# A row-maximum kernel that ignores NaN: ScalarE writes back part of each tile from the 31st to the 60th, and the last tiles are divided anew

## The chip, the cores and the metric

The kernel runs on one core of one Trainium2 chip. The metric is the device time of one execution in microseconds (us). A core has several engines that work side by side and wait for each other by semaphores: ScalarE (ACT in the profile), GpSimd (POOL), VectorE (DVE) and SyncE (SP), which here only issues transfers. TensorE is not used.

## What is computed

```python
def setup_inputs():
    batch, seq, dim = 32, 2048, 2048
    x = np.random.randn(batch, seq, dim).astype(np.float32)
    mask = np.random.rand(batch, seq, dim) < 0.1
    x[mask] = np.nan
    return {"x": x, "axis": -1}

def reference(x, axis):
    return np.nanmax(x, axis=axis).astype(np.float32)
```

There are 65536 rows of 2048 float32 values, a tenth of them NaN. The output is the largest value of each row with the NaNs left out. The input is 537 MB, the output 0.26 MB.

## The kernel before

**How the work is cut.** Each of the 128 partitions gets 512 rows. A unit of 512 values, a quarter of a row (`Q`), is the measure of everything: a partition has 2048 of them. They are worked on in 74 tiles; the first has 4 quarters, each other one 28 (seven rows). This text counts tiles from 1. The list `TILES` has one entry for each tile, with three lists in quarters:

- the loads: `[20, 8]` means that the tile comes by two transfers, of 20 and 8 quarters. Each load has 128 rows, one for each partition, and is issued by SyncE (line 316).
- the pieces, by which the NaNs are taken out. An entry is one ScalarE instruction that makes keys; a tuple is one key instruction whose result is then worked on in several parts. A positive number is written back by GpSimd, a negative one by ScalarE.
- the reduces: each is one instruction of VectorE over so many quarters.

So `([28], [7, 9, 12], [16, 12])` is one load, three keys, three write-backs by GpSimd and two reduces (of four rows and of three), and `([28], [9, 12, -7], [8, 20])` gives the last 7 quarters to ScalarE and reduces two rows and then five.

**What is done to a piece.** ScalarE reads the upper 16 bits of each float32 as an integer and makes a key from it by a Prelu (`kt<-xt`, line 222): the key of a NaN is such that the way back gives the upper half of minus infinity. The write-back computes `TOP - key` and stores it over the upper half, by GpSimd's tensor_scalar (`xt<-kt`, line 232) or by a ScalarE Copy (`xt<-kt`, line 222). The lower half stays where it is, so every number is as it was and every NaN is minus infinity. VectorE then takes the maximum over whole rows (line 239). A reduce that ends within a row leaves its value in the last element it read, and the next one, which waits for it, begins there:

```python
                            lo = done - 1 if done % D else done
```

**Buffers.** A tile lies in one of three buffers `xt`; the loads of a tile wait for the last reduce of the tile three before (`free`). Keys lie in three buffers `kt` of 12 quarters each. A piece that no longer fits goes to the next key buffer and waits until everything in it has been written back; if it is also the last piece of its tile, it waits for the buffer after that too:

```python
                        if at + c == sum(loads) * Q:

                            kold = kold + last(kfree[(key + 1) % NKEYS])
```

**Order of the work.** Every engine works in the order of the program, tile after tile, and waits only by semaphores. SyncE issues the loads in order, each on the next of 14 lanes; a lane's load also waits for the one that used it before. ScalarE does the key of a piece and then the write-backs that are held for it. A negative piece is written back at once after its own key; one that is written as a float (`-7.0`) is held until after the next key, except where it is the tile's last:

```python
                            held.append((at - c, at, key, kp, e_key, piece))
                            if not wait or at == sum(loads) * Q:
                                release()
```

Where a reduce needs one last piece from GpSimd and one from ScalarE, and nobody else needs these, both count up one semaphore (`joints`, a pair), and the reduce waits for it alone; tiles 70 to 73 have no such pairs (`APART`).

**The end.** The tiles form six groups (15, 15, 15, 15, 13 and 1 tiles), each with its own stretch of the output. After tile 60 one VectorE instruction (line 245, over 414 values of each partition) turns minus infinity into NaN for the rows of the first four groups; after tile 74 one does the last group's 7 values, and two GpSimd instructions (lines 260 and 274) do the fifth group's. SyncE then stores the six groups.

Of the kernel before, what the change touches and what calls it, by code (L numbers as in the profile page):

```python
# [20 lines left out]
    + [([28], [9, 12, -7], [8, 20])]  # L21
    + [([28], [7, 9, 12], [16, 12])] * 7
    + [([28], [9, 12, -7], [8, 20])]
    + [([28], [7, 9, 12], [16, 12])] * 7
    + [([28], [9, 12, -7], [8, 20])]
    + [([28], [7, 9, 12], [16, 12])] * 7
    + [([28], [9, 12, -7], [8, 20])]
    + [([28], [7, 9, 12], [16, 12])] * 7
    + [([28], [6, 10, 12], [16, 12])] * 3
    + [([28], [7, 9, 12], [16, 12])]  # L30
    + [([28], [6, 10, 12], [16, 12])] * 3
    + [([28], [7, 9, 12], [12, 16])] * 2
    + [([28], [7, 10, 11], [12, 16])]
    + [([28], [6, 10, 12], [16, 12])] * 3
    + [([28], [8, 11, 9], [8, 8, 12])]
    + [([20, 8], [11, -6, 6, 5], [16, 12])]
    + [([20, 8], [12, (-4, 7), 5], [8, 8, 12])]
    + [([17, 11], [12, (-4, 6), 6], [4, 12, 12])]
    + [([16, 12], [11, -5, 5, 7], [16, 12])]
    + [([13, 15], [9, -4, 7, 8], [12, 8, 8])]  # L40
    + [([14, 14], [9, -4, 4, 4, 7], [12, 8, 8])]
    + [([11, 10, 7], [5, 6, (-3, 7), 7], [4, 4, 4, 8, 8])]
    + [([11, 9, 8], [4, 7, (-2, 7), 6, -2], [4, 4, 4, 8, 8])]
    + [([8, 7, 6, 7], [3, 5, 7, (3, -3), 3, 4], [8, 4, 8, 8])]
    + [([6, 5, 6, 5, 6], [5, (5, -1), (-1, 5), 5, 3, 3], [4, 4, 4, 4, 4, 4, 4])]
    + [([5, 6, 5, 4, 4, 3, 1], [(-2, 3), 3, 3, (4, -1), 4, 4, -2.0, 2], [4, 4, 3, 1, 4, 4, 4, 4])]
    + [([4, 4, 3, 2, 4, 2, 3, 3, 3], [2, 2, 4, (-2.0, 1), 2, 3, 3, (-1, 2), (1, -1, 1), 2, -1.0], [4, 4, 4, 4, 4, 4, 4])]
)

GROUPS = [TILES[i : i + 15] for i in range(0, 60, 15)] + [TILES[60:73], TILES[73:]]  # L50
# [453 lines left out]
```

## Time and profile before

| | |
|---|---|
| median of 3 runs | 1252.54 us (1252.48 to 1253.04) |
| the profiled execution | 1252.48 us, its span 1250.7 us |
| loads | 105, 536.87 MB read, 429 GB/s over the span |
| DMA queue busy | 99.4% of the span |
| VectorE (DVE) | 1111.4 us busy, 179 instructions |
| ScalarE (ACT) | 965.6 us busy, 273 instructions |
| GpSimd (POOL) | 1168.5 us busy, 242 instructions |
| ScalarE's keys wait for loads | 257.9 us in 69 waits |
| VectorE waits for GpSimd | 128.1 us in 58 waits |
| last load landed, last reduce ended | 1242.24 us, 1247.91 us after the span's start |

Busy time is the sum of an engine's instructions, and a wait is idle time of an engine that ended when another engine or a load was done. The span runs from the first instruction of the program to the last; the execution's own time has 1.8 us beside it. A line of the groups or the timeline has the engine, the line of the helper that issues the instruction, what it writes and reads, and the shape; a timeline line merges neighbouring instructions of one kind (`x2`), gives their start and their time, and in brackets the idle time before them with what ended it.

### The profile page before, as it was taken

The numbers are of one execution on the slowest core, as the hardware profiler recorded it, in microseconds if no ns is written. First come the engines' busy times: TensorE is split into PE (matmuls) and PEld (weight loads), VectorE is DVE, ScalarE is ACT, GpSimd is POOL, SyncE is SP. The second block draws the span as 40 slices with busy tenths as digits, with TensorE's granted clock in tenths as the row PEclk, the third lists the DMA queues.
The fourth block names the chain that finished last, engine by engine and source line by source line (L and its number), as shares of the span: only waits on it lengthen the run. The fifth ranks groups of instructions, "written<-read, shape, count | busy, mean of one in ns | idle before, by whom it ended". The sixth has DMA issues, their size and how long they took to land.

```text
span 1250.7 us, 891 instructions
## 1 busy us (share of the span) xinstructions
DVE 1111.4 (89%) x179; ACT 965.6 (77%) x273; POOL 1168.5 (93%) x242
## 2 busy tenths in 40 slices
DVE  0888989888889888898988888998888899999999
ACT  3777887778777877788777877777777778999997
POOL 2999989998999899998999899999999999989998
DMA  9999999999999999999999999999999999999997
GB/s 415 440 418 433 440 440 438 413 440 440 440 433 418 440 440 438 429 424 440 440 436 424 431 440 438 436 424 433 440 438 435 422 436 436 425 434 429 431 428 301
DMA packets 15991, 537.20 MB, mean 430 GB/s; under 512 B 2544, under 2 KB 2544, under 8 KB 3568
## 3 DMA queue, kind: packets, MB, share of 16 engines
q1 hardware_dynamic: 15984, 537.14, 99.4%
q14 instruction: 7, 0.06, 0.0%
HBM read 536.87 MB, written 0.26 MB: 429 GB/s over the span
## 4 chain that ended last, share of the span: by engine, by line
DMA 40%; DVE 29%; POOL 22%; ACT 9%; issue 1%; SPq 0%
DMA xt<-in_x_dram 40%; DVE acc L239 29%; POOL xt L232 22%; ACT kt L222 8%; ACT xt L222 1%; SPq L316 0%; DVE acc L245 0%; SPq L499 0%; SPq L215 0%
## 5 line engine op out<-in xcount | busy, mean ns | idle before, releaser
L232 POOL TENSOR_SCALAR xt<-kt 128x3584 int16<-128x3584 uint16 (+11 forms) x236 | 1167.4, 4947 | 77.6 <-ACT kt L222 63.9
L239 DVE TENSOR_REDUCE acc<-xt 128x3 f32<-128x6144 f32 (+4 forms) x175 | 1107.5, 6379 | 135.6 <-POOL xt L232 128.1
L222 ACT ACTIVATE kt<-xt 128x3584 uint16<-128x3584 int16 (+9 forms) x247 | 913.4, 3734 | 278.0 <-DMA xt<-in_x_dram 257.9
L222 ACT ACTIVATE xt<-kt 128x512 int16<-128x512 uint16 (+6 forms) x24 | 52.8, 2202 | 0.7
L245 DVE SCALAR_TENSOR_TENSOR acc<-acc 128x414 f32<-128x414 f32 (+1 forms) x2 | 2.2, 1111 | 0.1
L222 ACT ACT_TABLE_LOAD x1 | 1.3, 1283 | 0.9 <-SPq L215 0.9
L239 DVE TENSOR_REDUCE xt<-xt 128x1 f32<-128x1536 f32 x1 | 1.7, 1743 | 0.0
L278 DVE MEMSET scalars<- 128x1 f32 x1 | 0.1, 59 | 1.0 <-SPq L215 1.0
L260 POOL TENSOR_SCALAR late<-acc 128x91 int32<-128x91 f32 x1 | 0.5, 549 | 0.1
L274 POOL TENSOR_TENSOR acc<-acc,late 128x91 int32<-128x91 int32 x1 | 0.3, 341 | 0.1
L485 POOL MEMSET const-float32-0.0<- 128x1 f32 x1 | 0.1, 98 | 0.2 <-issue 0.2
L222 ACT ACTIVATE scalars<-scalars 128x1 f32<-128x1 f32 x1 | 0.2, 203 | 0.0
L485 POOL MEMSET const-bfloat16-1.0<- 128x1 bf16 x1 | 0.1, 101 | 0.0
L485 POOL MEMSET const-uint8-127<- 128x1 uint8 x1 | 0.1, 101 | 0.0
L485 POOL MEMSET const-float32-1.0<- 128x1 f32 x1 | 0.1, 98 | 0.0
## 6 DMA issues: line engine op xcount, KB each, us to landing
xt<-in_x_dram SPq DMA_DIRECT2D x61, 7168.0 KB, 22.6
xt<-in_x_dram SPq DMA_DIRECT2D x2, 5120.0 KB, 17.4
xt<-in_x_dram SPq DMA_DIRECT2D x3, 2816.0 KB, 22.7
xt<-in_x_dram SPq DMA_DIRECT2D x4, 2048.0 KB, 22.3
xt<-in_x_dram SPq DMA_DIRECT2D x5, 1536.0 KB, 29.1
xt<-in_x_dram SPq DMA_DIRECT2D x2, 3584.0 KB, 24.8
xt<-in_x_dram SPq DMA_DIRECT2D x6, 1024.0 KB, 26.8
xt<-in_x_dram SPq DMA_DIRECT2D x3, 1792.0 KB, 30.1
```

The costliest lines, as they stand in the source:

```text
L222: lambda: nc.scalar.activation(**kw),
L232: lambda: nc.gpsimd.tensor_scalar(**kw),
L239: return order.add("dve", nc.vector, lambda: do(**kw), deps)
L245: lambda: nc.vector.scalar_tensor_tensor(out=acc, in0=acc, scalar=LEAST, in1=acc, op0=ALU.is_ge, op1=ALU.mult,),
L260: lambda: nc.gpsimd.tensor_scalar(out=none, in0=acc, scalar1=LEAST, scalar2=float(0x00400000), op0=ALU.is_lt, op1=ALU.mult,),
L274: lambda: nc.gpsimd.tensor_tensor(out=bits, in0=bits, in1=none, op=ALU.add),
L278: e_warm = order.add("dve", nc.vector, lambda: nc.vector.memset(warm, 1.0), [])
L485: nc = _bacc.Bacc("TRN2", target_bir_lowering=False, num_devices=1)
```

## The change

Only the list `TILES` is changed. There are again 74 tiles of the same sizes and the same groups.

- Tiles 31 to 38 become `[10, 12, -6]` with reduces `[8, 20]`, tiles 39 to 61 `[9, 12, -7]` with `[8, 20]` or `[4, 24]` (13 of them the latter): ScalarE writes back the last 6 or 7 quarters. Tiles 33 and 41 had `[9, 12, -7]` before. Some of the numbers are floats.
- Tiles 62 to 74 are divided into other pieces, other reduces and other loads. The loads of the whole kernel go from 105 to 118; tile 63 comes by one load instead of two, tiles 73 and 74 by 14 each instead of 7 and 9, some of them of one quarter (256 KB). The reduces of tiles 63 to 74 go from 52 to 58; tile 74 has 13 instead of 7, among them six rows that are reduced in two steps.

```diff
--- before.py
+++ after.py
@@ -21,30 +21,41 @@
     + [([28], [9, 12, -7], [8, 20])]
     + [([28], [7, 9, 12], [16, 12])] * 7
     + [([28], [9, 12, -7], [8, 20])]
-    + [([28], [7, 9, 12], [16, 12])] * 7
+    + [([28], [7, 9, 12], [16, 12])] * 5
+    + [([28], [10, 12, -6.0], [8, 20])] * 2
+    + [([28], [10, 12, -6], [8, 20])]
+    + [([28], [10, 12, -6.0], [8, 20])] * 2
+    + [([28], [10, 12, -6], [8, 20])]
+    + [([28], [10, 12, -6.0], [8, 20])]
+    + [([28], [10, 12, -6], [8, 20])]
+    + [([28], [9, 12, -7], [4, 24])]
+    + [([28], [9, 12, -7], [8, 20])] * 2
+    + [([28], [9, 12, -7], [4, 24])]
+    + [([28], [9, 12, -7.0], [8, 20])]
+    + [([28], [9, 12, -7], [4, 24])]
+    + [([28], [9, 12, -7.0], [4, 24])] * 3
+    + [([28], [9, 12, -7.0], [8, 20])]
+    + [([28], [9, 12, -7.0], [4, 24])]
+    + [([28], [9, 12, -7.0], [8, 20])] * 2
+    + [([28], [9, 12, -7.0], [4, 24])] * 4
+    + [([28], [9, 12, -7.0], [8, 20])] * 2
+    + [([28], [9, 12, -7.0], [4, 24])]
+    + [([28], [9, 12, -7], [4, 24])]
+    + [([28], [9, 12, -7.0], [8, 20])]
     + [([28], [9, 12, -7], [8, 20])]
-    + [([28], [7, 9, 12], [16, 12])] * 7
-    + [([28], [9, 12, -7], [8, 20])]
-    + [([28], [7, 9, 12], [16, 12])] * 7
-    + [([28], [6, 10, 12], [16, 12])] * 3
-    + [([28], [7, 9, 12], [16, 12])]
-    + [([28], [6, 10, 12], [16, 12])] * 3
-    + [([28], [7, 9, 12], [12, 16])] * 2
-    + [([28], [7, 10, 11], [12, 16])]
-    + [([28], [6, 10, 12], [16, 12])] * 3
-    + [([28], [8, 11, 9], [8, 8, 12])]
-    + [([20, 8], [11, -6, 6, 5], [16, 12])]
-    + [([20, 8], [12, (-4, 7), 5], [8, 8, 12])]
-    + [([17, 11], [12, (-4, 6), 6], [4, 12, 12])]
-    + [([16, 12], [11, -5, 5, 7], [16, 12])]
-    + [([13, 15], [9, -4, 7, 8], [12, 8, 8])]
-    + [([14, 14], [9, -4, 4, 4, 7], [12, 8, 8])]
-    + [([11, 10, 7], [5, 6, (-3, 7), 7], [4, 4, 4, 8, 8])]
-    + [([11, 9, 8], [4, 7, (-2, 7), 6, -2], [4, 4, 4, 8, 8])]
-    + [([8, 7, 6, 7], [3, 5, 7, (3, -3), 3, 4], [8, 4, 8, 8])]
-    + [([6, 5, 6, 5, 6], [5, (5, -1), (-1, 5), 5, 3, 3], [4, 4, 4, 4, 4, 4, 4])]
-    + [([5, 6, 5, 4, 4, 3, 1], [(-2, 3), 3, 3, (4, -1), 4, 4, -2.0, 2], [4, 4, 3, 1, 4, 4, 4, 4])]
-    + [([4, 4, 3, 2, 4, 2, 3, 3, 3], [2, 2, 4, (-2.0, 1), 2, 3, 3, (-1, 2), (1, -1, 1), 2, -1.0], [4, 4, 4, 4, 4, 4, 4])]
+    + [([28], [8, (4, -7.0), 9], [12, 16])]
+    + [([28], [5, 7, 10, 6], [4, 8, 8, 8])]
+    + [([16, 12], [(8, -4), 8, 8], [12, 8, 8])]
+    + [([12, 16], [(9, -3.0), 8, 8], [12, 8, 8])]
+    + [([16, 12], [(8, -4), 8, 8], [12, 8, 8])]
+    + [([13, 15], [8, -5, 8, 7], [12, 8, 8])]
+    + [([14, 14], [6, (-3, 5), 6, 8], [4, 8, 8, 8])]
+    + [([10, 12, 6], [(-3, 7), 5, (5, -1.0), 7], [8, 4, 8, 8])]
+    + [([9, 6, 5, 8], [8, 7, -5, 4, 4], [8, 12, 8])]
+    + [([7, 8, 6, 7], [(5, -2), (1, 2), 5, (-2, 4), 3, 4], [8, 4, 4, 8, 4])]
+    + [([5, 4, 7, 5, 4, 3], [5, (1, -3), 3, 4, 5, (2, -2.0), 3], [8, 4, 4, 4, 4, 4])]
+    + [([5, 2, 2, 1, 4, 1, 1, 2, 2, 2, 3, 1, 1, 1], [4, 3, (1, -1, -1.0), 3, 3, (-1.0, 3), 2, 2, (-1, 3)], [4, 4, 4, 4, 4, 4, 4])]
+    + [([3, 2, 3, 3, 2, 4, 1, 1, 1, 1, 1, 4, 1, 1], [2, 3, 3, 2, (-2, 1), 1, 1, 2, (1, 1, -1.0), 2, 2, (-1, 1, 1), -1.0], [2, 2, 1, 3, 4, 3, 1, 2, 2, 2, 2, 2, 2])]
 )
 
 GROUPS = [TILES[i : i + 15] for i in range(0, 60, 15)] + [TILES[60:73], TILES[73:]]
```

## The prediction

> **What bounds the kernel now.** I read the page first: busy shares and the rate of the loads.
>
> ```profile
> DVE 1111.4 (89%) x179; ACT 965.6 (77%) x273; POOL 1168.5 (93%) x242
> GB/s 415 440 418 433 440 440 438 413 440 440 440 433 418 440 440 438 429 424 440 440 436 424 431 440 438 436 424 433 440 438 435 422 436 436 425 434 429 431 428 301
> q1 hardware_dynamic: 15984, 537.14, 99.4%
> ```
>
> The load queue is never idle. 28 quarter rows (7.34 MB) take a steady 16.9 us, 0.604 us a quarter. So for most of the run nothing that the engines do can matter unless it takes over 16.9 us a tile or frees a buffer too late. The table by windows of 16.9 us shows where that changes (window, busy us of DVE, ACT and POOL with instructions, clock, DMA share, GB/s):
>
> ```profile
> 980.20:997.10 16.90, 15.14 (x3) 12.40 (x4) 16.44 (x4) 1.00 1.00 434
> 1081.60:1098.50 16.90, 16.90 (x5) 15.38 (x5) 16.13 (x4) 1.00 1.02 438
> 1216.80:1233.70 16.90, 16.87 (x10) 16.12 (x13) 16.27 (x9) 1.00 1.02 426
> 1233.70:1250.60 16.90, 14.38 (x8) 11.15 (x11) 11.84 (x11) 1.00 0.51 198
> ```
>
> VectorE is idle 1.8 us a window in the middle and not at all near the end. The timeline of the end says from when:
>
> ```profile
> 1032.58 2.06 DVE L245 SCALAR_TENSOR_TENSOR acc<-acc 128x414 f32<-128x414 f32 x1
> 1034.56 23.79 DVE L239 TENSOR_REDUCE acc<-xt 128x4 f32<-128x8192 f32 x4
> 1058.51 162.84 DVE L239 TENSOR_REDUCE acc<-xt 128x3 f32<-128x6144 f32 x40 [0.16 <-POOL xt L232]
> 1223.04 24.87 DVE L239 TENSOR_REDUCE acc<-xt 128x1 f32<-128x513 f32 x12
> 1247.94 0.17 DVE L245 SCALAR_TENSOR_TENSOR acc<-acc 128x7 f32<-128x7 f32 x1
> ```
>
> From tile 61's first reduce (1034.56) to the last (1247.91) VectorE stops for under 0.4 us. The last load lands at 1242.24, 5.7 us before. So: loads set the time up to tile 60, VectorE's unbroken row of reduces after it. The chain of waits at the end runs through GpSimd (1203.99 to 1236.83), but VectorE's idle time there is nil: the two are level.
>
> The third thing to read is what one tile of the new form costs; tile 9 already has it (9 and 12 quarters by GpSimd, 7 by ScalarE):
>
> ```profile
> 141.07 9.26 ACT L222 ACTIVATE kt<-xt 128x4608 uint16<-128x4608 int16 x2 [4.07 <-DMA xt<-in_x_dram]
> 145.19 12.46 POOL L232 TENSOR_SCALAR xt<-kt 128x4608 int16<-128x4608 uint16 x2 [1.02 <-ACT kt L222]
> 150.56 3.19 ACT L222 ACTIVATE kt<-xt 128x3584 uint16<-128x3584 int16 x1 [0.23 <-POOL xt L232]
> 153.78 4.20 ACT L222 ACTIVATE xt<-kt 128x3584 int16<-128x3584 uint16 x1
> 157.95 7.12 ACT L222 ACTIVATE kt<-xt 128x3584 uint16<-128x3584 int16 x2
> 158.02 10.82 DVE L239 TENSOR_REDUCE acc<-xt 128x5 f32<-128x10240 f32 x1 [1.46 <-ACT xt L222]
> 161.22 16.73 POOL L232 TENSOR_SCALAR xt<-kt 128x3584 int16<-128x3584 uint16 x3 [3.56 <-ACT kt L222]
> ```
>
> **Part 1: tiles 31 to 61.** -7 and -7.0 give the same order, since a last piece is always written back at once; 33 and 41 had ScalarE write back before, so 29 tiles change. (Times below count from the tile's landing, L.)
>
> ScalarE: 9.26 for the first two keys, 0.23 waiting for GpSimd to free a key buffer, 3.19, 0.03, 4.20: done at L+16.91. A following key can start 0.13 before a write-back ends (2.49 from 1093.42, next key at 1095.78), so 16.78 a tile against a load's 16.90. A 10, 12, -6 tile: 4.46 for the key of 10, then 6.04 until GpSimd's 10 quarters (5.90) are done, 2.76, 0.03, 3.63, less 0.13: 16.79. ScalarE just keeps up, at 99%. GpSimd falls from 16.7 to 12.5 a tile, worth nothing while the loads bind.
>
> VectorE: the work is the same; what matters is when the buffer comes free. 8, 20: the 20 starts at L+16.95 and ends at L+27.8 (now, with 16, 12: 118.34 - 90.25 = L+28.1). 4, 24: the 24 is not in the trace; 10.82 plus one row of 2.13 is 12.96, so L+29.9. The load three tiles on is issued then, with 33.8 - 29.9 = 3.9 us of the load before it still to come. The first load of the run needed 5.67 - 0.96 = 4.71 us from issue to landing, of which four quarters' transfer is 2.41: a lead of 2.3 us is enough. 3.9 covers it; uncovered, each of the 13 such tiles would cost what is missing. Part 1: 0.
>
> ScalarE: Activation LUTs of the Trainium skill (What ACT_TABLE_LOAD costs) gives an ACTIVATE 186 ns and 0.833 ns an element, by which the write-back of 3584 takes 3.17 and the tile 15.8, with a microsecond of slack. The row's 4.20 disagrees and decides; by either the loads bind.
>
> **Part 2: the hand-over, tiles 60 to 62.** Tile 59 (landing 987.34) ends on VectorE at 1017.2; tile 60's 8 runs to 1021.5, its 20 to 1032.3, the flag operation (2.06) to 1034.3, tile 61's 8 to 1038.6. Tile 61's 20 needs ScalarE at 1021.12 + 16.9 = 1038.0, so it runs 1038.6 to 1049.3 (before: 1049.69). Tile 62 (landing 1038.00): keys 8 and 11 end at 1046.4; the key of 9 waits for GpSimd's 8 (1041.72 + 4.77 = 1046.49) and ends at 1050.6; GpSimd's 9 ends at 1056.04. VectorE's 12 runs 1049.3 to 1055.8, its 16 from 1056.1 to 1064.8. Tile 63 starts about 1064.72 instead of 1065.07: **-0.35**.
>
> **Part 3: tiles 63 to 74 on VectorE.** The rows reduced are the same; their number goes from 52 to 58. Start to start, 8 quarters take 4.32 and two of 4 take 2 x 2.19, so a cut costs 0.06: 6 x 0.06 = **+0.36**. A row done in two reduces makes the second wait for the first: it starts 0.03 after the first's end (1223.01, 1223.04), where others start 0.085 before it. Six such rows against one: 5 x 0.115 = **+0.58**. That sum holds while the other two stay ahead. Going through these tiles with ACT, POOL and DVE durations by size, GpSimd is done with what VectorE needs next 0.2 to 1.5 us early nearly everywhere; the tightest are tile 62's 16 (above), tile 70's 8 (1170.8 against 1170.7) and, in tile 74, leads of 0.25 to 0.4. GpSimd's last piece ends about 1246.0, ScalarE's at 1245.8, VectorE's last reduce starts about 1247.2. GpSimd's relief (4.2 us of work fewer after tile 60) thus ends as idle time in tiles 66, 67, 70 and 72, where it waits for keys.
>
> **Part 4: thirteen more loads.** Landing to landing, one load takes 16.88 (tile 62), two 16.94 to 16.97, five 17.07, nine 17.25: 0.046 a load, 0.6 in all, so the last lands at about 1242.8. VectorE's row covers that with some 1 us; if the cover were gone, at most 0.6. The 13 issues on SP (0.43 each) sit behind the wait for tile 70's and 71's buffers, free at 1186 and 1201.5, needed at 1208 and 1225. SP stalled up to 5.16 us in such an issue (1202.01), with nine loads outstanding; nine of the new ones are still 14 quarters, 8 us of transfer. The four early stores follow later, but only after the last load, as now.
>
> Sum on the profiled run (1252.48 us; span 1250.7 and 1.8 around it): -0.35 + 0.36 + 0.58 = +0.6. The median of the runs is 1252.54, the same within 0.1. **Forecast 1253.1 us**, no difference by the 0.2% (2.5 us) that a measurement can tell.
>
> **Rivals.**
> - ScalarE becomes the pace in tiles 31 to 61 (slower). If back to back the next key starts 0.08 after the write-back instead of 0.13 before (that gap is GpSimd's), a tile takes 16.99, and 31 tiles lag 2.8 us; VectorE's 20 or 24 waits for it, so tile 62 starts that much later and all follows: 1252.5 + 0.6 + 2.8 = 1255.9. It decides above 16.90 a tile. For: 99% load, no two such tiles in a row in the trace. Against: the 0.13 overlap occurs after every write-back with its load landed. 0.10.
> - 4, 24 frees buffers too late: half a microsecond short in 13 tiles is 6.5 us, 1259.6. Against: 3.9 against 2.3. 0.03.
> - Each extra load pays its own latency (the 2.3 above less overlap, at least 1.3): 13 x 1.3 = 17 us, 1270. Against: nine loads cost 0.37 in tile 74. 0.02. DMA: Bandwidth & Descriptors of the Trainium skill (Rules for kernel authors) asks for 1 MiB or more per DMA; the new loads of one quarter are 256 KB. The one such load before landed 0.63 after its neighbour against 0.60, so by this trace the rule costs little in a full queue.
> - The end follows the last landing, VectorE having more slack than I see (faster): 1242.8 + key 0.61, write-back 0.78, a half-row reduce 1.2 and gaps is 1245.5, 2.4 before: 1250.0. For: the chain runs through GpSimd, which is relieved. Against: VectorE's unbroken row. 0.05.
>
> **Chances.** Forecast 0.80, mostly within 0.2%. Faster 0.04 (most of the last rival), same 0.81, slower 0.15 (the first three). Range: a microsecond and a half below for stops of the loads (16.99 to 17.38 us in a few tiles) that may fall otherwise, up to most of the first rival above: 1251.5 to 1255.3.
>
> **What would show it.** ScalarE's keys in tiles 40 to 60 starting on a landing, not on its own queue; tile 62's last reduce ending near 1064.8; VectorE without idle time after it; the last landing near 1242.8. Wrong if VectorE waits over a microsecond in tiles 63 to 74, or tile 61 lands past 1023.

## The result, and the profile after

The changed kernel takes 1258.38 us (median of 6 runs, 1256.79 to 1260.71) against 1252.47 (1252.40 to 1253.04): the ratio is 1.0049, with a 95% interval of 1.0037 to 1.0061. It is slower by 5.9 us, more than the 0.2% that was named, and outside the range of the prediction. The profiled execution is the slowest of the six: 1260.71 us, span 1258.9.

The page of the changed kernel, the lines that answer to those of before:

```profile
DVE 1115.6 (89%) x184; ACT 1086.4 (86%) x306; POOL 1050.6 (83%) x221
GB/s 412 437 437 435 434 415 435 438 438 437 434 421 428 437 437 437 437 435 437 434 423 428 437 437 434 432 430 430 428 423 426 437 434 404 432 435 428 427 423 261
q1 hardware_dynamic: 17856, 537.14, 99.1%
```

GpSimd's 118 us less and ScalarE's 121 us more are as the change says. VectorE has 4.2 us more. Line numbers of the changed kernel are 11 higher than before (L233 here is L222 there). The table by windows of the changed kernel:

```profile
980.20:997.10 16.90, 12.99 (x3) 16.63 (x5) 12.37 (x3) 1.00 1.00 434
1081.60:1098.50 16.90, 16.90 (x5) 14.78 (x5) 16.58 (x5) 1.00 1.03 445
1216.80:1233.70 16.90, 16.90 (x8) 15.85 (x15) 16.16 (x10) 1.00 1.03 420
1233.70:1250.60 16.90, 16.76 (x13) 15.86 (x16) 15.79 (x15) 1.00 0.83 327
```

VectorE is as full at the end as before, only later. The timeline of the changed kernel around tiles 60 and 61 has ScalarE's part as forecast and one line that was not:

```profile
1007.09 9.26 ACT L233 ACTIVATE kt<-xt 128x4608 uint16<-128x4608 int16 x2
1016.59 3.19 ACT L233 ACTIVATE kt<-xt 128x3584 uint16<-128x3584 int16 x1 [0.24 <-POOL xt L243]
1019.81 4.21 ACT L233 ACTIVATE xt<-kt 128x3584 int16<-128x3584 uint16 x1
1024.66 9.26 ACT L233 ACTIVATE kt<-xt 128x4608 uint16<-128x4608 int16 x2 [0.65 <-DMA xt<-in_x_dram]
1028.79 12.46 POOL L243 TENSOR_SCALAR xt<-kt 128x4608 int16<-128x4608 uint16 x2 [5.12 <-ACT kt L233]
1035.11 6.52 DVE L256 SCALAR_TENSOR_TENSOR acc<-acc 128x414 f32<-128x414 f32 x1
1041.55 36.70 DVE L250 TENSOR_REDUCE acc<-xt 128x2 f32<-128x4096 f32 x6
```

ScalarE ends tile 60 at 1024.02 and then waits 0.65 us for a load. So it keeps up, and it is the load that is late: tile 61 lands at 1024.64, before at 1021.12. And the flag operation, the VectorE instruction after tile 60 that turns minus infinity into NaN, took 2.06 us before and takes 6.52; that alone is as much as VectorE has more. Tile 61 also lands past the 1023 that the prediction named as a sign of being wrong. The end of the program on the same timeline:

```profile
1251.75 4.00 SPq L472 DMA_DIRECT2D out_dram<-acc  x2
1255.22 0.17 DVE L256 SCALAR_TENSOR_TENSOR acc<-acc 128x7 f32<-128x7 f32 x1
```

The two stores are merged in the first line. The second is issued at 1255.4, behind the last flag operation, and lands at 1257.76, 2.35 us later; before, that took 1.41.

Laid beside the trace of before, the 8.2 us by which the profiled span is longer (1258.9 - 1250.7) lie here:

| stretch | before | after | difference |
|---|---|---|---|
| start to the landing of tile 41 | 682.68 | 683.32 | +0.6 |
| to the landing of tile 61 | 338.44 | 341.32 | +2.9 |
| to the end of tile 61's last reduce | 28.57 | 32.05 | +3.5 |
| to the end of the last reduce of all | 198.22 | 198.50 | +0.3 |
| to the end of the program | 2.79 | 3.73 | +0.9 |

The first row has nothing of the change in it until tile 31, and loads there stop now and then in both kernels (tile 24 took 17.38 before, 17.69 after). The other rows are the questions for the experiments.

### The profile page after: what moved, and what is told of

The parts are those of the page before. It is cut to its first block, busy times and chain, and to the rows that moved or that the text cites. A ratio compares the mean times of both kernels' runs of the same rounds, so it can differ in the third digit from the quotient of the medians.

```text
span 1258.9 us, 936 instructions
## 1 busy us (share of the span) xinstructions
DVE 1115.6 (89%) x184; ACT 1086.4 (86%) x306; POOL 1050.6 (83%) x221
## 4 chain that ended last, share of the span: by engine, by line
DVE 34%; DMA 25%; ACT 23%; POOL 17%; issue 1%; SPq 0%
DVE acc L250 32%; DMA xt<-in_x_dram 25%; POOL xt L243 17%; ACT kt L233 16%; ACT xt L233 8%; DVE xt L250 1%; DVE acc L256 1%; SPq L327 0%; SPq L510 0%; SPq L226 0%
## 5 line engine op out<-in xcount | busy, mean ns | idle before, releaser
L250 DVE TENSOR_REDUCE acc<-xt 128x2 f32<-128x4096 f32 (+7 forms) x175 | 1102.2, 6350 | 138.7 <-POOL xt L243 92.9
L243 POOL TENSOR_SCALAR xt<-kt 128x6144 int16<-128x6144 uint16 (+9 forms) x215 | 1049.5, 4881 | 200.7 <-ACT kt L233 189.0
L233 ACT ACTIVATE kt<-xt 128x3584 uint16<-128x3584 int16 (+10 forms) x249 | 914.2, 3706 | 161.7 <-DMA xt<-in_x_dram 137.8
L233 ACT ACTIVATE xt<-kt 128x3584 int16<-128x3584 uint16 (+6 forms) x55 | 172.8, 3143 | 1.5
L250 DVE TENSOR_REDUCE xt<-xt 128x1 f32<-128x1024 f32 (+2 forms) x6 | 7.2, 1208 | 0.0
L256 DVE SCALAR_TENSOR_TENSOR acc<-acc 128x414 f32<-128x414 f32 (+1 forms) x2 | 6.7, 3344 | 0.1
L233 ACT ACTIVATE scalars<-scalars 128x1 f32<-128x1 f32 x1 | 0.2, 203 | 0.0
```

What stands on the lines that cost most here:

```text
L233: lambda: nc.scalar.activation(**kw),
L243: lambda: nc.gpsimd.tensor_scalar(**kw),
L250: return order.add("dve", nc.vector, lambda: do(**kw), deps)
L256: lambda: nc.vector.scalar_tensor_tensor(out=acc, in0=acc, scalar=LEAST, in1=acc, op0=ALU.is_ge, op1=ALU.mult,),
```

## The experiments

**Theories.** One: the flag operation waits for whichever GpSimd instruction is under way, and the change puts a longer one there. Two: a reduce of 24 quarters frees its buffer so late that the load queue loses time. Rival to both: ScalarE at 99%, or the new tail, is the loss. Times are medians; the kernel before, run beside them, had 1252.47 to 1252.57.

**Without the flag operation.** The first four groups keep minus infinity for a row that is all NaN.

```diff
-                e = find(after, accs[:, lo:flagged])
+                e = find(after, accs[:, lo:flagged]) if gi != 3 else after[-1]
```

> The changed kernel without the flag operation after tile 60 (rows that are all NaN in the first four groups would keep minus infinity; nothing else is left out). Theory 1, that this VectorE operation waits 6.1 us for GpSimd's instruction under way: tile 61's last reduce ends about 4 us earlier than in the changed kernel, and the time falls by 3 to 4.5 us to about 1254.5 (the late loads stay). Rival, that all of the loss is late loads: the operation's place is taken by idle time, within 1 us of 1258.4.

1255.74 us (1254.55 to 1257.78), ratio 1.0026 (1.0017 to 1.0035): 2.6 us less, under the 3 to 4.5 expected. In its trace VectorE waits 2.2 us for ScalarE where the flag was, and tile 61's last reduce ends 27.8 us after its landing instead of 32.0. That is the 4 us expected there, but VectorE then waits 0.6 us for GpSimd in tile 62, so not all of it reaches the end. The flag is real and not all; the scatter stays.

**8 and 20 quarters instead of 4 and 24**, in 13 tiles.

```diff
-    + [([28], [9, 12, -7.0], [4, 24])] * 3
+    + [([28], [9, 12, -7.0], [8, 20])] * 3
 ...
```

> The changed kernel with every reduce list of 4 and 24 quarters made 8 and 20 (13 tiles from 39 to 59), so that a buffer is free 2.1 us sooner. Theory 2, that loads issued under 4.3 us before the queue runs out make the queue lose time: tile 61 lands by about 1021.5 instead of 1024.6, and the time falls by 2 to 3.5 us to about 1255.5; the runs also lie closer together than the changed kernel's (1256.8 to 1260.7). Rival, that loads stop at random places whatever the lead: tile 61 as late as now, time within 1 us of 1258.4.

1256.93 us (1256.69 to 1257.33), ratio 1.0034 (1.0022 to 1.0046): 1.5 us less where 2 to 3.5 were expected, and the runs now lie within 0.6 us where the changed kernel's lay within 3.9. Tile 61 lands at 1021.39, as expected. Two windows of the changed kernel, each four tiles long:

```profile
752.00:820.00 68.00, 62.11 (x9) 66.69 (x17) 49.52 (x8) 1.00 0.99 427
888.00:956.00 68.00, 62.50 (x8) 66.19 (x16) 49.52 (x8) 1.00 1.01 427
```

and of this one:

```profile
752.00:820.00 68.00, 60.96 (x9) 66.91 (x17) 49.53 (x8) 1.00 1.00 433
888.00:956.00 68.00, 61.03 (x9) 66.90 (x17) 49.55 (x8) 1.00 1.00 432
```

The last number is the rate of the loads: 427 becomes 433 and 432, with ScalarE as busy as before the edit (66.9 of 68). ScalarE's load is therefore not what slowed the queue.

**Both edits.**

> Both edits: 8 and 20 in place of 4 and 24, and no flag operation after tile 60 (rows that are all NaN in the first four groups would keep minus infinity). If theories 1 and 2 are the whole loss: 1252 to 1253.2, level with the kernel before. If something else in the new tail costs too: above 1254.

1253.74 us (1253.54 to 1254.22), ratio 1.0010 (1.0001 to 1.0018). Flag and late loads are 4.6 of the 5.9 us. Something else is worth 1.2; it was not in the 1252 to 1253.2 that was expected.

**Late buffers in the kernel before**, with ScalarE's and GpSimd's work untouched: 14 of the tiles from 34 to 48 reduce 8 and then 20 quarters.

```diff
-    ([28], [7, 9, 12], [16, 12]),
+    ([28], [7, 9, 12], [8, 20]),
 ...
```

> The kernel before with one thing changed: in 14 of the tiles 34 to 48 the reduces are 8 and 20 quarters instead of 16 and 12, so that a tile's buffer comes free 2.8 us later (31 us after its landing instead of 28), with the same ScalarE and GpSimd work. Theory 2: a load is issued some 3 us before the queue runs out instead of 5.7, the queue loses 0.3 to 1 us for each, 4 to 12 us in all: 1257 to 1265. Rival, that the late loads come from ScalarE's work or from chance: under 1 us, 1252.5 to 1253.5.

1261.22 us (1260.17 to 1263.72), ratio 1.0073 (1.0061 to 1.0086): 8.7 us for 14 tiles, 0.62 each. Two windows of this kernel:

```profile
684.00:752.00 68.00, 58.35 (x9) 54.00 (x13) 60.42 (x12) 1.00 0.99 420
752.00:820.00 68.00, 58.70 (x8) 49.79 (x12) 64.38 (x12) 1.00 0.98 418
```

and the same of the kernel before:

```profile
684.00:752.00 68.00, 60.95 (x9) 54.34 (x14) 62.44 (x12) 1.00 1.00 433
752.00:820.00 68.00, 60.95 (x9) 50.16 (x13) 66.67 (x13) 1.00 1.00 433
```

The late buffer alone does it, and no engine has more to do.

**GpSimd's 12 quarters of tile 61 in two instructions**, the flag operation where it was.

```diff
-    ([28], [9, 12, -7], [8, 20]),
+    ([28], [9, 6, 6, -7], [8, 20]),
```

> The changed kernel with GpSimd's 12 quarters of tile 61 in two instructions of 6 (keys too); the flag operation after tile 60 stays where it is. If it waits for the GpSimd instruction under way and gets in between two: it ends 0.4 us after the first 6 quarters, 3 us instead of 6.5, and the time falls by 2 to 3.5 us to about 1255.5. Rival, that 414 values with two inputs simply take that long, or that the operation waits until GpSimd has nothing left: 6.5 us as now, 1258.4.

1255.43 us (1254.82 to 1256.83), ratio 1.0024 (1.0014 to 1.0035): as good as leaving the flag out. Its timeline:

```profile
1026.75 12.90 POOL L275 TENSOR_SCALAR xt<-kt 128x4608 int16<-128x4608 uint16 x3 [4.44 <-ACT kt L265]
1033.79 2.38 DVE L288 SCALAR_TENSOR_TENSOR acc<-acc 128x414 f32<-128x414 f32 x1
```

GpSimd's three instructions are merged in the first line; the second of them ends at 1035.80. The flag operation ends at 1036.18, 0.38 later: it got in between two GpSimd instructions.

**The flag operation one reduce later.**

```diff
-                e = find(after, accs[:, lo:flagged])
-                ready += [e] * (gi + 1 - len(ready))
+                if gi == 3:
+                    moved.append((after, accs[:, lo:flagged]))
 ...
                             after.append(e)
+                            if moved:
+                                ready += [find(*moved.pop())] * 4
```

> The changed kernel with the flag operation of the first four groups issued one reduce later, after tile 61's first reduce instead of before it. VectorE then would wait for ScalarE's write-back anyway until 0.35 us after GpSimd's 12 quarters are done. If the flag's cost is only its wait for GpSimd: the same as without it, 1255.7 (1254.5 to 1257.8, the late loads stay). If its cost is its own work: 1258.4.

1255.73 us (1254.34 to 1258.04), ratio 1.0026 (1.0015 to 1.0037): the same as without it, though it runs.

```profile
1027.01 12.48 POOL L243 TENSOR_SCALAR xt<-kt 128x4608 int16<-128x4608 uint16 x2 [4.71 <-ACT kt L233]
1037.95 1.92 DVE L256 SCALAR_TENSOR_TENSOR acc<-acc 128x414 f32<-128x414 f32 x1
1039.86 10.82 DVE L250 TENSOR_REDUCE acc<-xt 128x5 f32<-128x10240 f32 x1
```

GpSimd ends at 1027.01 + 12.48 = 1039.49, the flag at 1039.88, again 0.39 us later, when VectorE could have begun its reduce anyway. The same 0.38 to 0.39 us after the end of the GpSimd instruction under way is found for this flag in all fifteen kernels of this study that have it.

**New middle, old tail; old middle, new tail.**

```diff
-TILES = (tiles 1 to 61 and 62 to 74 of one kernel)
+TILES = (tiles 1 to 61 of one, 62 to 74 of the other)
 ... (in words)
```

> Tiles 1 to 61 as in the changed kernel, 62 to 74 with the loads, pieces and reduces of before. Of the loss of 5.9 us the middle and the hand-over (late loads 1.5 to 2, flag 2.6 to 3.2) stay and the new tail's share (1.2) goes: about 1257.2. If the new tail is what makes up for something, above 1258.4.

1256.49 us (1255.48 to 1258.35), ratio 1.0034 (1.0021 to 1.0046), a little under the 1257.2 expected: the old tail saves 1.9.

> Tiles 1 to 61 as before, 62 to 74 with the loads, pieces and reduces of the changed kernel. My prediction's sum for the tail alone, six more reduces and five more rows in two steps, is 0.9 less what tile 62 gives: 1253.0 to 1253.9, VectorE's last reduce ending 0.5 to 0.9 later than before. If the thirteen loads cost on the path, the last landing passes 1243.5 and the time 1254.5.

1253.82 us (1253.48 to 1254.14), ratio 1.0010 (1.0001 to 1.0019). The new tail costs 1.25 us by itself. In its trace the last load lands at 1242.66 and the last reduce ends at 1248.30, 0.4 later than before (1247.91); but the last store takes 2.2 us from issue to landing instead of 1.4.

**Only the new loads, only the old loads.** The kernel before with the loads of the new tail, and the new tail with the old loads.

```diff
-    ([20, 8], [11, -6, 6, 5], [16, 12]),
+    ([28], [11, -6, 6, 5], [16, 12]),
 ...
```

> The kernel before with only the loads of tiles 62 to 74 of the changed kernel (118 instead of 105), pieces and reduces as before. My prediction: nothing on the path, 1252.5 to 1252.9. Rival, from the traces of the kernels with the new tail, where the last store needs 2.0 to 2.35 us from issue to landing instead of 1.4: the number of loads does this, 0.5 to 0.9 slower, 1253.1 to 1253.5, with the last reduce ending where it did.

1256.13 us (1256.02 to 1256.67), ratio 1.0029 (1.0018 to 1.0041): a miss, both readings were too low. VectorE's timeline:

```profile
1066.38 8.69 DVE L282 TENSOR_REDUCE acc<-xt 128x4 f32<-128x8192 f32 x1 [1.36 <-POOL xt L275]
1075.60 6.55 DVE L282 TENSOR_REDUCE acc<-xt 128x3 f32<-128x6144 f32 x1 [0.53 <-POOL xt L275]
1083.32 17.40 DVE L282 TENSOR_REDUCE acc<-xt 128x2 f32<-128x4096 f32 x4 [1.17 <-POOL xt L275]
```

Tile 63's first piece had begun when 20 quarters were there; now it waits for all 28, and VectorE loses 3.1 us that it never gets back. A tail's loads and pieces only work as a pair.

> Tiles 1 to 61 as before, 62 to 74 with the pieces and reduces of the changed kernel but the loads of before (105). If the number of loads makes the last store late: 1.4 us from its issue to its landing, and 1252.7 to 1253.2 (VectorE's longer row of reduces alone). If the late store comes from something else in the tail: 1253.8, as with all 118 loads. Some pieces wait longer for a larger load, which could add up to 0.5.

1255.86 us (1255.76 to 1256.43), ratio 1.0027 (1.0016 to 1.0038): a miss too, 2.0 us over the same tail with its own loads. The other way round the same happens: VectorE waits 1.1, 1.2 and 0.3 us in tile 70, whose first load has 11 quarters where its pieces were cut for 9. The time says nothing of the store, but the trace does. The lines of the last store (engine, count, size, median us from issue to landing), first with the new loads in the old tail, then with the old loads in the new tail:

```profile
out_dram<-acc SPq DMA_DIRECT2D x1, 3.5 KB, 2.0
```
```profile
out_dram<-acc SPq DMA_DIRECT2D x1, 3.5 KB, 1.4
```

In all kernels of this study with 118 loads it is 1.96 to 2.35 us, in all with 105 loads 1.40 to 1.41.

**Tile 74 in whole rows.**

```diff
-[2, 2, 1, 3, 4, 3, 1, 2, 2, 2, 2, 2, 2]
+[4, 4, 4, 4, 4, 4, 4]
```

> Tiles 1 to 61 as before, 62 to 74 as in the changed kernel, except that tile 74 is reduced in 7 whole rows instead of 13 steps. By the sum of the prediction six cuts (0.36) and six waits of a second step (0.69) go: VectorE's last reduce ends about 1 us earlier than with 13 steps, less what the last row waits for its last quarter; time 1252.8 to 1253.3 against 1253.8. If the steps are hidden: 1253.8.

1254.51 us (1254.23 to 1255.12), ratio 1.0016 (1.0007 to 1.0025): 0.7 slower than with 13 steps, against the expectation.

```profile
1232.63 6.67 DVE L282 TENSOR_REDUCE acc<-xt 128x1 f32<-128x2048 f32 x3 [0.73 <-POOL xt L275]
1239.97 9.01 DVE L282 TENSOR_REDUCE acc<-xt 128x1 f32<-128x2048 f32 x4 [0.68 <-POOL xt L275]
```

A whole row must wait for its last quarter, 0.73 and 0.68 us; the steps start on half a row at once. They cost more work and give back more waiting.

**Number or nearness of the loads.** The kernel before with 13, 7 or 1 of its tiles from 19 on loaded in two halves; one execution each.

```diff
-    ([28], [7, 9, 12], [16, 12]),
+    ([14, 14], [7, 9, 12], [16, 12]),
 ...
```

> The kernel before with tiles 19 to 31 loaded in two transfers of 14 quarters each instead of one of 28: 118 loads, the tail as before. If the number of transfers makes the last store land late: 2.0 us or more from its issue to its landing. If the small loads near the end do: 1.4 us. The loads themselves: 13 x 0.046 = 0.6 us later at the end by the price that the prediction used.

> The same with tiles 19 to 25 in two loads: 112. By the number of transfers, something else than 1.4 us from the last store's issue to its landing, if the effect grows or steps with it; by nearness 1.4 us.

> The same with tile 19 alone in two loads: 106. Close to the kernel before: 1.4 us by either reading, unless the effect depends on the exact number.

The last store's line for 118, 112 and 106 loads:

```profile
out_dram<-acc SPq DMA_DIRECT2D x1, 3.5 KB, 2.1
```
```profile
out_dram<-acc SPq DMA_DIRECT2D x1, 3.5 KB, 1.5
```
```profile
out_dram<-acc SPq DMA_DIRECT2D x1, 3.5 KB, 1.4
```

With the added loads 900 us before the end it is 2.1 all the same. So it goes with how many transfers came before, not with small ones being near. The traces narrow it further. The store's packets (the pieces that the DMA engines move) end 1.03 us after its issue in all kernels, with 105 loads and with 118, and the first of the sixteen counts that tell of its landing follows at 1.23 to 1.24; only later counts come late. The store just before it, of 45.5 KB and with 122 transfers ahead of it, takes 1.53 to 1.74 us with 118 loads and 1.57 to 1.61 with 105, so it shows no such step. The times of these three kernels (1254.36, 1252.97 and 1253.12 us) are too few to say more.

**A version from all this**: the new middle with 8 and 20 throughout, the flag moved, the old tail.

> A version made from what the runs showed: the middle of the changed kernel with 8 and 20 quarters throughout (no late loads), the flag operation behind tile 61's first reduce, and tiles 62 to 74 as before. Late loads, the flag's wait, the extra steps and the thirteen loads are all gone; tile 61's last reduce ends 0.5 to 0.9 earlier than in the kernel before, part of which tile 62 loses again to GpSimd: 1251.9 to 1252.6, level with or a little under the kernel before (1252.5). If ScalarE at 99% in the middle costs something that I do not see: 1253 or more.

1252.69 us (1252.51 to 1253.10), ratio 1.0000 (0.9991 to 1.0009): level, just above the 1251.9 to 1252.6 expected. Its tile 61 is done sooner after landing than before, but VectorE then waits 0.96 us for GpSimd in tile 62. No version tried beats the kernel before.

## Why the prediction was wrong

- **The hand-over, the flag's term: wrong, 2.6 to 3.2 us.** I carried the flag over at 2.06 us as if it were work. The row itself spoke against that: 414 values took 2.06, while a reduce of 513 takes 0.69. It was a wait that looks like busy time. VectorE reaches the operation when forecast (1032.33 with 8 and 20 throughout, 1032.3 was worked out); its length is what was wrong, 6.05 there. The operation asks at 1035.11 while GpSimd's 12 quarters run from 1034.21 to 1041.25; before, it asked at 1032.58, and GpSimd's 10 quarters ended at 1034.25. Removing it, splitting GpSimd's instruction and moving it each gave the time back. At tile 61 it costs 4.2 us, and 2.6 to 3.2 of them reach the end. The Trainium skill has the rule, in SBUF — State Buffer (section Who interferes with whom): VectorE instructions with two SBUF inputs and GpSimd instructions that read SBUF take turns on a shared port, and the loser stands still for the whole instruction of the other. This operation reads `acc` twice. The traces here agree: the operation ended 0.38 to 0.39 us after GpSimd's in every kernel that has it. I did not weigh that rule.
- **Part 1, "a lead of 2.3 us is enough": wrong, 1.5 to 2.0 us.** The lead is the time from a load's issue to the landing of the load before it. It was 3.8 to 4.2 in nine of the thirteen loads, about the 3.9 worked out, and it was not enough: of these, the loads of tiles 42, 48 and 49 landed on time (16.90 to 16.92 us after the one before), those of 45, 47, 50, 55, 56 and 61 took 17.15 to 17.58. The other four, with 4.4 to 5.0, were on time. Tile 51 took 17.60 with a lead of 6.1; it stops in the kernel with 8 and 20 too (17.25), so that is not all the lead's. The trace's packets (here one partition's 28 quarters each) show how one load's latency at the start misleads. The first packets of a tile start 1.4 us and more before the tile ahead has landed, as the 16 engines don't finish together; so 3.9 us leaves 2.5 at most from the issue to the first packet, and there some first packets took 2.3 to 3.7 us instead of 2.12. Why they are slower is not shown; the four loads that landed on time with 4.4 to 5.0 have a few such packets too. The rival with this mechanism stood at 0.03; its price of 0.5 a tile was too high for these tiles (0.11 to 0.15 on the mean of 13) and nearly right where about 3 us are left (0.62). That its 1259.6 is near the measured 1258.38 is luck: about half of the loss is the flag.
- **Part 1, ScalarE: right.** It keeps up at 16.8 us a tile; in the changed kernel its keys of tile 60 still start 0.02 us after the landing, after twenty such tiles, and so they do with 8 and 20, where late loads give ScalarE no rest. The first rival did not come.
- **Part 3, VectorE's sum: nearly right.** With the old middle and the new tail VectorE never waits over 0.1 us after tile 61. It is 0.68 us ahead of the kernel before at the end of tile 73 and 0.39 behind at the end of tile 74. So tile 74, with its six more reduces and six rows in two steps, costs 1.07, against 0.36 + 0.58 in the sum. With flag and late loads gone the last reduce ends at 1248.49, +0.6 on 1247.91. That is the forecast's number, but partly by luck: without the flag tile 61 ends 0.95 earlier than before instead of 0.39, and VectorE then waits 0.6 for GpSimd in tile 62 and 0.3 in tile 70, the places that the prediction called tightest. The term of +0.58 does not stand for a loss that one could have back: whole rows wait longer.
- **Part 4, thirteen loads: right on the queue, wrong on the end.** The last load lands at 1242.66 with the new tail, 1242.8 was forecast. What the sum put at nothing, a change in the time from the last store's issue to its landing, is 0.5 to 0.9.
- **The run-to-run spread** of the changed kernel, 3.9 us, comes with the late loads: it is 0.6 with 8 and 20.

In medians: late loads 1.5, the flag 3.2 (1256.93 - 1253.74) and the new tail about 1.2 make 5.9. Taken out in the other order, the flag is 2.6 and the late loads 2.0. The tail's 1.2 is split by traces alone: VectorE's longer row 0.4 to 0.6, the last store 0.5 to 0.8.

## What to carry to other kernels

Read a short operation's duration against its size before carrying it over: where it takes far longer than a larger operation of the same engine (here 2.06 us for 414 values against 0.69 for 513), it may hold a wait, and the wait depends on what runs beside it. Where a load queue is the bound, the time from a buffer's release to the queue's running dry is a resource of its own: an edit that leaves every engine's work alone can spend it. Counted to the landing of the load ahead it looks larger than it is, since the next load's first packets start earlier, by 1.4 us and more here. Loads and the pieces cut from them are one design; changing the loads alone cost 3.6 us in the old tail and 2.0 in the new one.

## What the runs showed of the hardware

- The one VectorE operation with two inputs here, the flag, issued while a GpSimd instruction was under way, ended 0.38 to 0.39 us after the end of that instruction in fifteen kernels, for waits of 1.5 to 6.1 us; a gap of 0.08 us between two GpSimd instructions was enough for it to get in.
- The queue lost nothing with a load of 28 quarters issued 5 us or more before the tile ahead had landed, beyond stops of 0.2 to 0.8 us that are there in every run, mostly at the same tiles (16, 24 and 51 or 57). With 3.8 to 4.2 us it lost 0 to 1.1 at a time, with 2.9 to 3.3 up to 2.0. The spread is wide: one such load of 3.1 us lost nothing.
- The same 3.5 KB store lands 1.4 us after its issue when 110 or 111 transfers went before it, 1.5 after 117 and 2.0 to 2.35 after 123, though its packets end 1.03 us after the issue each time. The number of transfers goes with it, not the place of the added ones; why is open.
